# Three chunks instead of two taken in turns at the start of two stages, with later norm sums and fewer small VectorE operations

## The chip, the cores and the metric

The kernel runs on one core of a Trainium2 chip. The metric is the device time of one execution in microseconds; lower is better. The core's engines are named as in the profile: PE is TensorE (matrix products), PEld its weight loads, DVE is VectorE, ACT is ScalarE, POOL is GpSimd, and SP issues most of the transfers.

## What is computed

The reference is a chain of residual blocks on x of 256 tokens by 1024 channels, all in float32: a gated linear attention, a feed-forward network and a gated side input (PLE), then a differential attention, a second feed-forward network and PLE, then a short convolution and a blockwise attention (MoBA). The change touches the differential attention and the convolution. Cut to what matters:

```python
def diff_attn_mixer(h, pos, w_in, g_q, g_k, lam_q1, lam_k1, lam_q2, lam_k2, g_sub, w_out, lambda_init):
    q, k, v = split_cols(h @ w_in, [D_MODEL, D_MODEL, D_MODEL])
    q = rms_norm(q.reshape(bsz, seq, nh, 2, dh), g_q)
    k = rms_norm(k.reshape(bsz, seq, nh, 2, dh), g_k)
    ...
    lam = (jnp.exp(jnp.sum(lam_q1.astype(F32) * lam_k1.astype(F32)))
           - jnp.exp(jnp.sum(lam_q2.astype(F32) * lam_k2.astype(F32))) + lambda_init)
    ...
        s = jnp.einsum('bhtqd,bhtkd->bhtqk', q_blk, kt).astype(F32) * scale
        pr = jax.nn.softmax(s, axis=-1)
        a = pr[:, :, 0] - lam * pr[:, :, 1]
        return jnp.einsum('bhqk,bhkd->bhqd', a.astype(vt.dtype), vt)
    ...
    o = rms_norm(o, g_sub) * (1.0 - lambda_init)
    return o.reshape(bsz, seq, D_MODEL) @ w_out

def short_conv_mixer(h, w_in, conv_w, w_out):
    b_gate, c_gate, xv, z = jnp.split(h @ w_in, 4, axis=-1)
    u = c_gate * xv
    ...
    y = b_gate * conv * jax.nn.silu(z)
    return y @ w_out
```

`h` is `rms_norm` of the block's input each time: x times the inverse root of its mean square, times a gain. There are 8 heads of two halves of 64.

## The kernel before, in words

**Products.** Each matrix product in float32 is made of three on split numbers: the left and right side are cut into a high part (a cast, `whi`, `xh`) and the rest (`wlo`, `xl`), and high by high, high by low and low by high are summed in one bank (`mm3`, L222 to L225). A *chunk* is 256 output columns; its 1024 inputs are 8 groups of 128. A chunk is cut into two *halves* of four groups each, 24 matmuls of TensorE. A half is one unit of the list `seq`, and one *turn* of the program.

**A turn.** `turn` (L196) first does side work that is due, then calls `ahead` (L160): the transfer of a unit's weights on SP's queue (512 KB into one of four buffers `raw`), the cast to `whi` on ScalarE (L169), the subtract to `wlo` on VectorE (L178), four to five units ahead of their use; then more side work; then the 24 matmuls. Side work is kept in a heap by due time in turns; the delays stand in the table `DL`, by step name and, where a chunk or norm has its own, its number. Each engine carries out its instructions in the order in which the program issues them, so the table sets what stands behind what.

**Banks.** Three banks of the accumulator (pool `psg`, names `g`) hold chunks in work, five (`psm`, names `m`) all else. A chunk's bank is free when the engines that read it are done.

**The norm ahead of a stage.** The norm's gain is applied to the input at once, its inverse root only when a chunk is read out, so products start before the root is known. Each quarter i of the input (two groups of 128) gives `xh` (ScalarE, L301), `xl` (VectorE, L305), a square (ScalarE, L314) and sums of squares (L321 and L325 on GpSimd, L329 on VectorE). `fin` (L338, L343) sums over the channels with a matmul of ones; `root` (L348) loads ScalarE's table of exponential and logarithm and makes `rb` (and per token `rn`, `ev` at L357). The quarters come from the chunks of the PLE in front: its `done` (L453 reads the bank, a tanh at L457, a product with `pj` at L461, a sum `h` at L466). The differential attention's norm is number 3, the convolution's number 6.

**Order at a stage's beginning.** `woven` takes the first chunks in turns: first halves, then second halves. The second half of any chunk needs the last quarters of the input, which the last PLE chunk makes.

```python
    def woven(chunks, n=2):

        r = [u for p in zip(*chunks[:n]) for u in p]
        return r + [u for c in chunks[n:] for u in c]
```

**Differential attention** (`diff_plan`). Chunks q0, k0, q1, k1, q2, k2, v0, q3, k3, v1, v2, v3; a q or k chunk carries two heads. `qk_done` reads its bank: products with the tables `qcos` and `qsin` (or k's) on VectorE (L888, L893), their sum `ro` on GpSimd (L897), a square on ScalarE (L795), sums `ss` and `ms` on VectorE (L799, L801), their inverse root `r` on ScalarE (L282, L283). k is scaled by `r` on GpSimd (L901); for q, `r` is kept as two scaled copies `rqs` (L904, L905). Transposes on TensorE (L818) and a split into high and low (`kh` L823, `kl` L829) follow. `scores` takes a head through products on TensorE, a maximum (L941) and `nb` (L943) on VectorE, exponentials on ScalarE (L951), the weights `w` (L959 to L961) and the mix of the two softmaxes `e` (L968) on VectorE, transposes of it on TensorE (L975). `lam` makes the factor lambda, with the exponential `le` on ScalarE (L876) from VectorE's `ls` (L874).

**pT.** `proj_units` loads `pT` (128 rows of 512 numbers, 256 KB) for the second PLE's projection: one transfer on ScalarE's queue (L420), one cast to `px` (L427) and one subtract (L424).

**Convolution** (`conv_plan`). Sixteen chunks by the same `gemm` and `woven`; `cs` is the delay of a silu of the odd chunks.

Of the kernel before, what the change touches and what calls it, by code (L numbers as in the profile page):

```python
# [12 lines left out]
F32 = mybir.dt.float32  # L13
# [3 lines left out]
ALU = mybir.AluOpType  # L17
AX = mybir.AxisListType

P = 128  # L20
# [32 lines left out]
for _name, _n in (("ident", 128), ("dmask", 64)):  # L53
# [16 lines left out]
    "grm.2": 1.25, "grm.3": 1.75, "grh": 0, "grl": 0.75, "gload": 20.75, "dlam": 15.25, "dload": 24, "dqadd": 0,  # L70
    "dkadd": 0, "dqsq": 1, "dqred": 0, "dqrt": 0.75, "dqr": 0.5, "dqr.2": 1.25, "dqtr": 0, "dqhi": 0, "dqlo": 0.75,
    "dksq": 0, "dkred": 0, "dkrt": 0.75, "dkr": 0, "dktr": 1.25, "dkhi": 0, "dklo": 0.25, "dsc0": 0.75,
# [3 lines left out]
    "cs": 3.25, "cs.7": 2, "cy1": 0, "cy2": 0.75, "ch": 0, "cl": 2.25, "mqsq": 0, "mqred": 0.75, "mqrt": 0.5,  # L76
# [19 lines left out]
def body(ctx: ExitStack, tc: tile.TileContext, a, out: bass.AP):  # L96
# [269 lines left out]
    proj, hpj = {}, {}  # L366
# [108 lines left out]
    def ffn_plan(layer):  # L475
        p = 3 * layer + 1
        N = norms[p]
        S = SimpleNamespace(act={})

        def done(ps, f):  # L480
            g, sg, t3 = t1(), t1(), t1()
            nc.vector.tensor_mul(g, ps[:, 0], N.rb)  # L482
            if f < 8:
                if f % 2 == 0:
                    S.spare = new_x()
                ah, al = S.spare[0][:, f % 2], S.spare[1][:, f % 2]
            else:
                ah, al = [S.fp.tile([P, T], F32R, tag=n, name=n, bufs=FT - 8) for n in ("ah", "al")]

            def lo():  # L490
                nc.vector.tensor_sub(al, t3, ah.bitcast(F32))
                S.act[f] = (ah, al)

            chain(layer, ("fs", lambda: nc.scalar.activation(sg, g, AF.Silu)),  # L494
                  ("fm", lambda: nc.vector.tensor_mul(t3, sg, ps[:, 1])),
                  ("fh", lambda: nc.scalar.copy(ah, t3)),
                  ("fl", lo))

        ins = [gemm([("ffn_i", layer * FT + f, HALVES)], N.xs, lambda ps, f=f: done(ps, f)) for f in range(FT)]
        outs = [gemm([("ffn_o", (layer * 4 + i) * 3 + c, n) for c, n in enumerate((HALVES, HALVES, (4, 2)))], S.act,  # L500
                     lambda ps, i=i: add_h(p, i, ps, N.rb)) for i in range(4)]

        @contextmanager
        def room():
            with tc.tile_pool(name=f"ff{layer}", bufs=1) as S.fp:
                yield

        return woven(ins) + [u for c in outs for u in c], room
# [335 lines left out]
    def diff_plan():  # L844
        N = norms[3]
        S = SimpleNamespace(og={}, rq={}, qT={}, kT={}, aT={}, tabs={}, el={}, vd=set())
        load, proj_u = proj_units(1)
# [37 lines left out]
        def qk_done(ps, i, nm):  # L885
# [13 lines left out]
            def by_r():  # L899
                if nm == "k":  # L900
                    on("dkn").tensor_mul(units64(b.ro), units64(b.ro), per64(b.r))  # L901
                else:
                    sc = S.gt.tile([P, 2, 2, 4], F32, tag="rqs", name="rqs", bufs=3)
                    nc.vector.tensor_scalar(sc[:, 0], b.r, 0.125, None, op0=ALU.mult)  # L904
                    nc.vector.tensor_scalar(sc[:, 1], b.r, -0.125, None, op0=ALU.mult)  # L905
# [20 lines left out]
        def scores(h):  # L926
# [12 lines left out]
            def top(c):  # L939
                mx = tiny.tile([P, 2], F32, tag="mx", name="mx")  # L940
                nc.vector.tensor_reduce(mx, b.ps[c], axis=AX.X, op=ALU.max)  # L941
                nb = tiny.tile([P, 2], F32, tag="nb", name="nb", bufs=3)
                nc.vector.tensor_mul(nb, mx, S.rq[i][:, 1, :, 2 * hl + c])  # L943
                b.nb.append(nb)

            def exps(c):
# [3 lines left out]
                for t in range(2):  # L950
                    nc.scalar.activation(e[:, t], b.ps[c][:, t], AF.Exp, bias=b.nb[c][:, t:t + 1],  # L951
                                         scale=S.rq[i][:, 0, t, 2 * hl + c:2 * hl + c + 1],
# [3 lines left out]
            def weights():  # L956
# [3 lines left out]
                nc.vector.tensor_mul(b.w, b.w, b.l[:, 0])  # L960
                nc.vector.tensor_scalar(b.w, b.w, S.nlam, None, op0=ALU.mult)  # L961
# [72 lines left out]
        units = woven([q(0), k(0), q(1), k(1), q(2), k(2), v(0), q(3), k(3), v(1), v(2), v(3)])  # L1034
# [3 lines left out]
        def room():  # L1038
            with tc.tile_pool(name="diff", bufs=1) as S.gp, tc.tile_pool(name="difft", bufs=1) as S.gt:
                prepare()  # L1040
                at("dload", load)
# [5 lines left out]
    def conv_plan():  # L1047
        p = 6
# [67 lines left out]
        return ple_plan(1) + woven(chunks) + out_chunks("conv_o", S.ys, p, lambda: N.rb), room  # L1116
# [311 lines left out]
```

## Time and profile before

| | |
|---|---|
| median of 3 runs | 938.64 us (937.6 to 939.99) |
| the profiled execution's own time | 937.24 us |
| its span, first to last instruction | 935.1 us |
| mean granted clock of TensorE in it | 0.992 |
| instructions in the span | 19090 |

The span is the part that the views show; the 2.1 us around it are start and end. Times in the views count from the span's start. A wait is put down to the engine, tile and line that ended last of all that an instruction waited for. TensorE's instructions overlap, so a row's own duration is longer than the step from one start to the next.

### The profile page before, as it was taken

Reading aid. Unit: us, or ns where it says so; the run is one execution under the profiler, and the core shown is the slowest. Engines: PE = TensorE matmul, PEld = TensorE weight load, DVE = VectorE, ACT = ScalarE, POOL = GpSimd, SP = SyncE. Lnnn points to the kernel's source line nnn. Section 1 sums busy time; section 2 is a strip of 40 time slices with the busy share of each in tenths; the row PEclk is TensorE's granted clock in tenths of the full one; section 3 lists DMA queues with packets and bytes.
Section 4 is the critical chain, followed back from the end, with each engine's and each line's share of the span. In section 5 each row is a group of like instructions: output and inputs, shape, how many; then the busy total and the mean of one; then the engine's idle time right before and its main releaser. Section 6 shows DMA issues by size and latency. Waiting matters only on the chain.

```text
span 935.1 us, 19090 instructions
## 1 busy us (share of the span) xinstructions
PE 913.7 (98%) x7812; PEld 900.6 (96%) x7812; DVE 663.4 (71%) x1000; ACT 556.2 (59%) x951; POOL 107.3 (11%) x74
## 2 busy tenths in 40 slices
PE   9889999999999989899999999999999999999998
PEld 8889999999999989899999999999999999999998
DVE  5884768666656698998587666566897668876663
ACT  5945757455444565677585545444774445777862
POOL 0050310000001352211010000012210003000010
PEclk9989999999999998999999999999999999999999
DMA  8543366655555734343466555565556546644332
GB/s 243 200 138 107 109 205 230 211 189 195 181 189 190 241 127 149 122 141 108 146 217 215 199 193 193 177 200 195 168 206 201 192 132 205 186 134 136 113 114 90
DMA packets 48151, 161.10 MB, mean 172 GB/s; under 512 B 5472, under 2 KB 6368, under 8 KB 48064
## 3 DMA queue, kind: packets, MB, share of 16 engines
q1 hardware_dynamic: 47376, 158.81, 51.7%
q8 instruction: 61, 1.00, 0.4%
q10 hardware_dynamic: 688, 1.07, 0.4%
q14 instruction: 26, 0.21, 0.1%
HBM read 158.81 MB, written 1.05 MB: 171 GB/s over the span
## 4 chain that ended last, share of the span: by engine, by line
PE 81%; DVE 10%; ACT 4%; POOL 2%; issue 2%; DMA 2%; SPq 0%; ACTq 0%; POOLq 0%; DVEq 0%
PE g L223 25%; PE g L225 24%; PE g L224 24%; DVE wlo L178 3%; ACT whi L169 1%; PE m L223 1%; PE m L818 1%; DVE xl L305 1%; PE m L996 1%; DMA h<-in_xT 1%; PE m L1196 1%; PE m L653 1%; ACT xh L301 1%; PE m L224 1%; DVE q L600 1%
## 5 line engine op out<-in xcount | busy, mean ns | idle before, releaser
L223 PE MATMUL g<-xh,whi 128*128 128x256 f32 (+1 forms) x1672 | 465.7, 279 | 1.3 <-ACT whi L169 0.7
L225 PE MATMUL g<-xh,wlo 128*128 128x256 f32 (+1 forms) x1672 | 462.5, 277 | 0.2
L224 PE MATMUL g<-xl,whi 128*128 128x256 f32 (+1 forms) x1672 | 462.4, 277 | 0.1
L178 DVE TENSOR_TENSOR wlo<-raw,whi 128x1024 fp32r<-128x1024 f32 (+2 forms) x315 | 377.3, 1203 | 80.3 <-PE g L225 43.8
L169 ACT CAST whi<-raw 128x1024 fp32r<-128x1024 f32 (+2 forms) x315 | 312.0, 996 | 117.6 <-PE g L224 93.4
L223 PEld LDWEIGHTS g<-xh,whi 128*128 128x128 f32 (+1 forms) x1672 | 314.1, 188 | 2.4 <-ACT whi L169 1.0
L225 PEld LDWEIGHTS g<-xh,wlo 128*128 128x128 f32 (+1 forms) x1672 | 313.8, 188 | 0.6 <-DVE wlo L178 0.6
L224 PEld LDWEIGHTS g<-xl,whi 128*128 128x128 f32 (+1 forms) x1672 | 313.7, 188 | 0.6 <-DVE xl L305 0.3
L223 PE MATMUL g<-whi,xh 128*128 128x256 f32 x448 | 130.8, 292 | 3.5 <-ACT xh L301 3.5
L225 PE MATMUL g<-whi,xl 128*128 128x256 f32 x448 | 127.1, 284 | 0.2 <-DVE xl L305 0.2
L224 PE MATMUL g<-wlo,xh 128*128 128x256 f32 x448 | 126.9, 283 | 0.0
L223 PEld LDWEIGHTS g<-whi,xh 128*128 128x128 f32 x448 | 86.8, 194 | 5.2 <-ACT xh L301 4.0
L225 PEld LDWEIGHTS g<-whi,xl 128*128 128x128 f32 x448 | 86.6, 193 | 0.6 <-DVE xl L305 0.6
L224 PEld LDWEIGHTS g<-wlo,xh 128*128 128x128 f32 x448 | 86.5, 193 | 0.0
L494 ACT ACTIVATE t<-t 128x256 f32<-128x256 f32 x44 | 18.5, 420 | 85.7 <-DVE t L482 85.6
L223 PE MATMUL g<-ah,whi 128*128 128x256 f32 x224 | 61.8, 276 | 0.0
L224 PE MATMUL g<-al,whi 128*128 128x256 f32 x224 | 61.8, 276 | 0.0
L225 PE MATMUL g<-ah,wlo 128*128 128x256 f32 x224 | 61.8, 276 | 0.0
L482 DVE TENSOR_TENSOR t<-g,rb 128x256 f32<-128x256 f32 x44 | 18.6, 424 | 52.1 <-PE g L225 52.0
L305 DVE SCALAR_TENSOR_TENSOR xl<-h,small,xh 128x256 fp32r<-128x256 f32 x64 | 36.6, 610 | 17.1 <-ACT xh L301 17.1
L301 ACT ACTIVATE xh<-h,small 128x256 fp32r<-128x256 f32 x64 | 29.3, 503 | 32.1 <-DVE h L466 7.9
L379 POOL TENSOR_TENSOR h<-h,pj 128x512 f32<-128x512 f32 x8 | 12.9, 1621 | 276.6 <-DVE h L395 270.8
(224 smaller groups left out, 1010.0 us busy)
## 6 DMA issues: line engine op xcount, KB each, us to landing
raw<-in_ffn_i SPq DMA_DIRECT2D x88, 512.0 KB, 4.6
raw<-in_ffn_o SPq DMA_DIRECT2D x40, 512.0 KB, 4.0
raw<-in_conv_i SPq DMA_DIRECT2D x32, 512.0 KB, 4.6
raw<-in_moba_i SPq DMA_DIRECT2D x32, 512.0 KB, 3.8
raw<-in_diff_i SPq DMA_DIRECT2D x24, 512.0 KB, 3.8
raw<-in_gla_i SPq DMA_DIRECT2D x23, 512.0 KB, 5.1
raw<-in_ple_g SPq DMA_DIRECT2D x16, 512.0 KB, 4.7
raw<-in_gla_o SPq DMA_DIRECT2D x5, 512.0 KB, 4.0
```

What stands on the lines that cost most here:

```text
L169: nc.scalar.copy(hi[:, :kn * c], raws[u][:, :kn * c])
L178: nc.vector.tensor_sub(lo[:, :kn * c], raws.pop(u)[:, :kn * c], hi[:, :kn * c].bitcast(F32))
L223: nc.tensor.matmul(ps, lh, rh, start=first, stop=False, **kw)
L224: nc.tensor.matmul(ps, lh, rl, start=False, stop=False, **kw)
L225: nc.tensor.matmul(ps, ll, rh, start=False, stop=last, **kw)
L301: nc.scalar.activation(xh[:, j], h[:, j], AF.Copy, scale=gain[j])
L305: nc.vector.scalar_tensor_tensor(xl[:, j], h[:, j], gain[j], xh[:, j].bitcast(F32), op0=ALU.mult, op1=ALU.subtract)
L379: nc.gpsimd.tensor_add(n, h, proj[p // 3][i])
L482: nc.vector.tensor_mul(g, ps[:, 0], N.rb)
L494: chain(layer, ("fs", lambda: nc.scalar.activation(sg, g, AF.Silu)), ("fm", lambda: nc.vector.tensor_mul(t3, sg, ps[:, 1])), ("fh", lambda ...
L600: nc.vector.tensor_mul(Q[:, :, 0::2], q16.rearrange("p (m n) c -> p m n c", n=2), ep.rearrange("p (m n) c -> p m n c", n=2))
L653: nc.tensor.matmul(ps[:, d, :192], S.kk[d].rearrange("p (m n) c -> p m (n c)", n=2)[:, 2 * h + t], S.q3[d][:, 2 * h + t].rearrange("p n c ...
```

## The change

`woven` gets a third chunk in the differential attention (q0, k0 and q1) and in the convolution (the first three). `fin` of norms 3 and 6 is due a turn later. The load of `pT` for the second PLE, with its cast and subtract, is due 48 turns into the first feed-forward network, not 24 turns after the differential attention's beginning. Three delays move by a half or a whole turn. In the attention the maximum is taken with its sign turned, so that one copy of `rqs` serves for two; the two operations on `w` become one.

```diff
-"fin": 2, "fin.0": 1,
+"fin": 2, "fin.3": 3, "fin.6": 3, "fin.0": 1,
-"dload": 24,
+"dload": 48,
-"dsc0": 0.75, "dsc1": 1.75, "cs": 3.25, "cs.7": 2,
+"dsc0": 0.75, "dsc0.0": 1.25, "dsc1.0": 2.25, "dsc1": 1.75, "cs": 3.25, "cs.7": 2, "cs.0": 2.25,
...
@@ ffn_plan, room
             with tc.tile_pool(name=f"ff{layer}", bufs=1) as S.fp:
+                if layer == 0:
+                    at("dload", early["load"])
                 yield
@@ diff_plan
-        load, proj_u = proj_units(1)
+        early["load"], proj_u = proj_units(1)
...
-                    sc = S.gt.tile([P, 2, 2, 4], F32, tag="rqs", name="rqs", bufs=3)
-                    nc.vector.tensor_scalar(sc[:, 0], b.r, 0.125, None, op0=ALU.mult)
-                    nc.vector.tensor_scalar(sc[:, 1], b.r, -0.125, None, op0=ALU.mult)
+                    sc = S.gt.tile([P, 2, 4], F32, tag="rqs", name="rqs", bufs=3)
+                    nc.vector.tensor_scalar(sc, b.r, 0.125, None, op0=ALU.mult)
...
-                nc.vector.tensor_reduce(mx, b.ps[c], axis=AX.X, op=ALU.max)
+                nc.vector.tensor_reduce(mx, b.ps[c], axis=AX.X, op=ALU.max, negate=True)
...
                 nc.vector.reciprocal(b.w, b.l[:, 1])
-                nc.vector.tensor_mul(b.w, b.w, b.l[:, 0])
-                nc.vector.tensor_scalar(b.w, b.w, S.nlam, None, op0=ALU.mult)
+                nc.vector.scalar_tensor_tensor(b.w, b.w, S.nlam, b.l[:, 0], op0=ALU.mult, op1=ALU.mult)
...
-        units = woven([q(0), k(0), q(1), k(1), q(2), k(2), v(0), q(3), k(3), v(1), v(2), v(3)])
+        units = woven([q(0), k(0), q(1), k(1), q(2), k(2), v(0), q(3), k(3), v(1), v(2), v(3)], 3)
...
                 prepare()
-                at("dload", load)
                 yield
@@ conv_plan
-        return ple_plan(1) + woven(chunks) + out_chunks("conv_o", S.ys, p, lambda: N.rb), room
+        return ple_plan(1) + woven(chunks, 3) + out_chunks("conv_o", S.ys, p, lambda: N.rb), room
```

How the change moves instructions shows in the engines' queues. TensorE's, behind the two first halves of q0 and k0, before: `g_4333` is q0's bank and `g_4385` k0's, `m_4440` and `m_4442` the norm's sums; each half's 24 matmuls are cut to its first.

```order
L223 MATMUL g_4333<-whi_4237,xh_4292 128x256 [waits Activation_49]
L224 MATMUL g_4333<-wlo_4285,xh_4292 128x256 [waits DVE_49]
L225 MATMUL g_4333<-whi_4237,xl_4293 128x256 [waits DVE_49]
...
L338 MATMUL m_4440<-ssum_4301,ones_89 128x256 [waits DVE_49]
L343 MATMUL m_4442<-ones_89,ssum_4301 128x4 x2
L223 MATMUL g_4385<-whi_4283,xh_4292 128x256
```

And with the change, where `g_4422` is q1's bank, `g_4339` q0's and `g_4391` k0's:

```order
L223 MATMUL g_4422<-whi_4243,xh_4235 128x256 [waits DVE_49]
L224 MATMUL g_4422<-wlo_4291,xh_4235 128x256
L225 MATMUL g_4422<-whi_4243,xl_4236 128x256
...
L223 MATMUL g_4339<-whi_4289,xh_4298 128x256 [waits Activation_49]
L224 MATMUL g_4339<-wlo_4335,xh_4298 128x256
L225 MATMUL g_4339<-whi_4289,xl_4299 128x256
...
L338 MATMUL m_4477<-ssum_4307,ones_89 128x256 [waits DVE_49]
L343 MATMUL m_4479<-ones_89,ssum_4307 128x4 x2
L223 MATMUL g_4391<-whi_4333,xh_4298 128x256
```

q1's first half, on the first two quarters of the input, now stands ahead of q0's second half and waits for VectorE; the sum stands behind q0's second half as before, with one half more ahead of it.

ScalarE's queue around the root of the norm, before (`r_4549` belongs to q0, `r_4553` to k0; two products of the square at L795 stand between):

```order
L169 CAST whi<-raw 128x1024 x2
L348 ACT_TABLE_LOAD
...
L169 CAST whi<-raw 128x1024 x2
L795 ACTIVATE t_4529<-g 128x512
L795 ACTIVATE t_4537<-g 128x512
L169 CAST whi<-raw 128x1024
...
L283 ACTIVATE r_4549<-ln 128x8
...
L283 ACTIVATE r_4553<-ln 128x8
L876 ACTIVATE le<-ls 128x2
```

And with the change, whose lines 795 and 876 are 797 and 878:

```order
L169 CAST whi<-raw 128x1024 x3
L348 ACT_TABLE_LOAD
...
L169 CAST whi<-raw 128x1024 x2
L797 ACTIVATE t_4565<-g 128x512
L797 ACTIVATE t_4573<-g 128x512
L878 ACTIVATE le<-ls 128x2
L169 CAST whi<-raw 128x1024
...
L283 ACTIVATE r_4596<-ln 128x8
...
L283 ACTIVATE r_4600<-ln 128x8
```

Three casts, not two, stand ahead of the table load; `le` stands ahead of a cast and of the roots of q0 and k0, not behind them.

VectorE's queue around the same root, before:

```order
L329 TENSOR_TENSOR ssum<-ssum,sq 128x256 x2
L178 TENSOR_TENSOR wlo<-raw,whi 128x1024 x2
L357 TENSOR_SCALAR ev<-m 128x2
L178 TENSOR_TENSOR wlo<-raw,whi 128x1024
L888 TENSOR_TENSOR m<-g,qcos 128x512
L893 TENSOR_TENSOR m<-g,qsin 128x8x32 x2
```

And with the change:

```order
L329 TENSOR_TENSOR ssum<-ssum,sq 128x256 x2
L178 TENSOR_TENSOR wlo<-raw,whi 128x1024 x3
L357 TENSOR_SCALAR ev<-m 128x2
L178 TENSOR_TENSOR wlo<-raw,whi 128x1024
L890 TENSOR_TENSOR m<-g,qcos 128x512
L895 TENSOR_TENSOR m<-g,qsin 128x8x32 x2
```

One subtract more stands ahead of `ev`. From the first q product to the mix of head 2 (the third at L968) there are ten of these subtracts before and nine with the change.

## Rows read from the trace of the kernel before

**Rows 1.** The page, parts 1 and 2: engines' busy time, TensorE's clock by slices
```profile
PE 913.7 (98%) x7812; PEld 900.6 (96%) x7812; DVE 663.4 (71%) x1000; ACT 556.2 (59%) x951; POOL 107.3 (11%) x74
...
PEclk9989999999999998999999999999999999999999
```

**Rows 2.** Waits of TensorE, whole span: us in total, times, longest
```profile
PE g L223 <- ACT xh L301: 4.1, 3, 2.9
...
PE m L818 <- POOL ro L901: 1.9, 1, 1.9
...
PE m L224 <- DVE kl L829: 1.0, 1, 1.0
...
PE m L975 <- DVE e L968: 0.7, 1, 0.7
```

**Rows 3.** Timeline of TensorE, 338 to 352: start us, us, instruction [idle before <-releaser]
```profile
338.81 0.28 PE L223 MATMUL g<-whi,xh 128*128 128x256 f32 x1
...
345.76 0.28 PE L225 MATMUL g<-whi,xl 128*128 128x256 f32 x1
348.92 0.39 PE L223 MATMUL g<-whi,xh 128*128 128x256 f32 x1 [2.88 <-ACT xh L301]
...
350.89 1.17 PE L338 MATMUL m<-ssum,ones 128*128 128x256 f32 x2
```

**Rows 4.** Windows: us, busy us (instructions) by engine, granted clock, DMA, GB/s
```profile
350.50:357.30 6.80, 6.80 (x32) 6.58 (x31) 5.75 (x9) 5.53 (x9) 0.57 (x1) 0.50 0.54 184
```

**Rows 5.** Windows, the stretch behind it
```profile
355.30:401.54 46.24, 42.49 (x355) 40.63 (x354) 44.02 (x89) 28.88 (x69) 12.59 (x9) 0.98 0.39 127
```

**Rows 6.** Timeline of VectorE, 345 to 403
```profile
345.64 0.75 DVE L453 TENSOR_TENSOR t<-g,rb 128x256 f32<-128x256 f32 x2
...
354.17 1.22 DVE L178 TENSOR_TENSOR wlo<-raw,whi 128x1024 fp32r<-128x1024 f32 x1
355.30 0.68 DVE L888 TENSOR_TENSOR m<-g,qcos 128x512 f32<-128x512 f32 x1
...
399.95 1.66 DVE L968 SCALAR_TENSOR_TENSOR e<-e,w 128x256 f32<-128x256 f32 x2
```

**Rows 7.** Timeline of ScalarE, 349 to 353
```profile
349.70 1.98 ACT L169 CAST whi<-raw 128x1024 fp32r<-128x1024 f32 x2
351.69 1.28 ACT L348 ACT_TABLE_LOAD   x1
```

**Rows 8.** Groups of VectorE's instructions, 353 to 470: line, shapes, count | busy us, mean ns | idle
```profile
L961 DVE TENSOR_SCALAR w<-w,nlam 128x2 f32<-128x2 f32 x8 | 4.7, 584 | 0.3
...
L960 DVE TENSOR_TENSOR w<-w,l 128x2 f32<-128x2 f32 x8 | 1.3, 161 | 0.3
...
L905 DVE TENSOR_SCALAR rqs<-r 128x8 f32<-128x8 f32 x4 | 0.7, 162 | 0.0
```

**Rows 9.** Timeline of VectorE and GpSimd, 376 to 385
```profile
376.64 1.29 POOL L897 TENSOR_TENSOR ro<-m 128x512 f32<-128x512 f32 x1 [6.04 <-DVE w L959]
...
376.78 1.19 DVE L961 TENSOR_SCALAR w<-w,nlam 128x2 f32<-128x2 f32 x1
...
384.18 0.23 DVE L961 TENSOR_SCALAR w<-w,nlam 128x2 f32<-128x2 f32 x1
```

**Rows 10.** Timeline of TensorE and VectorE, 679 to 685, conv's beginning
```profile
679.03 0.75 DVE L453 TENSOR_TENSOR t<-g,rb 128x256 f32<-128x256 f32 x2
...
681.51 0.28 PE L225 MATMUL g<-xh,wlo 128*128 128x256 f32 x1
...
682.37 0.38 PE L223 MATMUL g<-xh,whi 128*128 128x256 f32 x1 [0.58 <-ACT xh L301]
...
684.28 0.70 PE L338 MATMUL m<-ssum,ones 128*128 128x256 f32 x2
```

**Rows 11.** Timeline of ScalarE, 362 to 366
```profile
362.79 0.21 ACT L283 ACTIVATE r<-ln 128x8 f32<-128x8 f32 x1
365.06 0.20 ACT L876 ACTIVATE le<-ls 128x2 f32<-128x2 f32 x1 [2.06 <-DVE ls L874]
```

More of the change, by code (lines that the diff above doesn't have):

```diff
@@ L69 @@
     "gon": 1.25, "gor": 0, "gom": 0, "grs.0": 4, "grs.1": 3, "grs.2": 2.75, "grs.3": 1, "grm.0": 1.5, "grm.1": 1.5,
-    "grm.2": 1.25, "grm.3": 1.75, "grh": 0, "grl": 0.75, "gload": 20.75, "dlam": 15.25, "dload": 24, "dqadd": 0,
+    "grm.2": 1.25, "grm.3": 1.75, "grh": 0, "grl": 0.75, "gload": 20.75, "dlam": 15.25, "dload": 48, "dqadd": 0,
     "dkadd": 0, "dqsq": 1, "dqred": 0, "dqrt": 0.75, "dqr": 0.5, "dqr.2": 1.25, "dqtr": 0, "dqhi": 0, "dqlo": 0.75,
-    "dksq": 0, "dkred": 0, "dkrt": 0.75, "dkr": 0, "dktr": 1.25, "dkhi": 0, "dklo": 0.25, "dsc0": 0.75,
+    "dksq": 0, "dkred": 0, "dkrt": 0.75, "dkr": 0, "dktr": 1.25, "dkhi": 0, "dklo": 0.25, "dsc0": 0.75, "dsc0.0": 1.25, "dsc1.0": 2.25,
     "dsc1": 1.75, "dp1": 0, "dt0": 0, "dt0.7": 0.25, "dt1": 0, "de0": 0.5, "de1": 0, "dw": 0.5, "dmix": 0.75,
@@ L75 @@
     "dored": 0, "dort": 0.5, "don": 0, "dotr": 1.25, "dohi": 0, "dolo": 0.25, "c0": 0, "c1": 1.75, "c2": 0,
-    "cs": 3.25, "cs.7": 2, "cy1": 0, "cy2": 0.75, "ch": 0, "cl": 2.25, "mqsq": 0, "mqred": 0.75, "mqrt": 0.5,
+    "cs": 3.25, "cs.7": 2, "cs.0": 2.25, "cy1": 0, "cy2": 0.75, "ch": 0, "cl": 2.25, "mqsq": 0, "mqred": 0.75, "mqrt": 0.5,
     "mqrt.0": 1.25, "mqn": 0.5, "mqtr": 0.75, "mqhi": 0.25, "mqlo": 1.25, "mksq": 0, "mkred": 0.25, "mkred.2": 0,
@@ L365, in body @@
     hs = [{} for _ in range(9)]
-    proj, hpj = {}, {}
+    proj, hpj, early = {}, {}, {}
     def give(p, i, h):
@@ L940, in top @@
                 mx = tiny.tile([P, 2], F32, tag="mx", name="mx")
-                nc.vector.tensor_reduce(mx, b.ps[c], axis=AX.X, op=ALU.max)
+                nc.vector.tensor_reduce(mx, b.ps[c], axis=AX.X, op=ALU.max, negate=True)
                 nb = tiny.tile([P, 2], F32, tag="nb", name="nb", bufs=3)
-                nc.vector.tensor_mul(nb, mx, S.rq[i][:, 1, :, 2 * hl + c])
+                nc.vector.tensor_mul(nb, mx, S.rq[i][:, :, 2 * hl + c])
                 b.nb.append(nb)
@@ L951, in exps @@
                     nc.scalar.activation(e[:, t], b.ps[c][:, t], AF.Exp, bias=b.nb[c][:, t:t + 1],
-                                         scale=S.rq[i][:, 0, t, 2 * hl + c:2 * hl + c + 1],
+                                         scale=S.rq[i][:, t, 2 * hl + c:2 * hl + c + 1],
                                          accum_out=b.l[:, c, t:t + 1])
```

2 rows, old and new, of the table DL are left out of this document.

## Prediction

> **What bounds the kernel now.** I read the engines and the clock by slices first, then TensorE's waits, then the two places that the change touches. TensorE is busy for 98% of the span, and two slices show a lower granted clock [rows 1]: time can only come from where TensorE stands or runs slowly. Of its waits, the largest, 2.9 us, is for ScalarE's `xh` (L301), and three shorter ones (1.9, 1.0, 0.7) are for GpSimd's `ro`, VectorE's `kl` and VectorE's `e` [rows 2]. TensorE's order of time puts the 2.9 where the differential attention begins: the two first halves of q0 and k0 run from 338.81, q0's second half stops after 345.76 and goes on at 348.92, since its last four inputs come from the last PLE chunk; the norm's sum stands at 350.89 [rows 3]. [...] From 355.30 to 401.54 another engine sets the pace: VectorE is busy for 44.02 of 46.24 us [rows 5]. The three shorter waits lie in it: TensorE is early there, and waits. So what TensorE wins before 355 reaches the end only as far as VectorE gets through its queue sooner.
>
> **The third first half.** Before, TensorE lost 348.92 - 345.76 = 3.16 us, 3.04 beyond one step of 0.118. Now q1's first half stands ahead of q0's second. It could start where two halves end, 338.81 + 48 x 0.118 = 344.47. But there are three banks, and q1 takes the one of the last PLE chunk, which VectorE reads out (L453) from 345.64 for 0.75 [rows 6]; in VectorE's queue all that stands ahead of this is unchanged. So the half waits some 2.0 us, starts at 346.45 and ends at 349.3 (24 x 0.118 = 2.83). By then `xh` is there (348.92 before), q0's second half runs through, and the sum comes at 352.1: four halves by 352.1, not three by 350.89, so TensorE is 2.83 - 1.2 = 1.6 us ahead. At most it wins 1.6, the 3.4 that the half clock cost (6.80 / 2), and the 3.6 of the shorter waits: 8.6. A part goes back at once, by my estimate under 1 us: with three chunks begun all three banks are taken until q0's is read out, and that ends after the first q products (356.25, below, with 0.68 and 0.75 for them, and ScalarE's square behind its casts), while k0 and q1 end at 352.4 + 2 x 2.83 = 358.1.
>
> **What VectorE makes of it.** Its first work on q0 waits for the norm's root, and that for ScalarE. There a cast more (1.98 for two, so 0.95 from start to start with overlap) stands ahead of the activation table load of 1.28 at 351.69 [rows 7]; that puts the load at 352.6, past the sum at 352.1 + 0.4. So `ev` and the first q product come 0.95 later, 356.25. Against this, to the mix of head 2 (399.95, the last that TensorE waits for here [rows 6]) the new queue has one `wlo` fewer: the third one is done before the root, where VectorE idles. That is 355.30 - 354.17 = 1.13. The trims: each q chunk loses one `rqs` (0.16), each head one of the two operations on `w` (0.16) [rows 8]; two and three of them stand ahead of head 2's mix, 0.80; one more of each ahead of k2's `kl`, 0.32. `negate` in the maximum adds an option, no instruction; its price no row shows: zero to 0.16 on each of 16 is its bound, and I take zero, since row for row a reduce costs its 512 elements. Sum: 0.95 - 1.13 - 0.80 - 0.32 = **-1.3 us**.
>
> **The merged operation on `w`.** At 376.78 the removed-in-part `w<-w,nlam` took 1.19, at 384.18 it took 0.23; the long one lies beside GpSimd's `ro`, 376.64 to 377.93 [rows 9]. Its mean of 584 ns over eight [rows 8] says that this happens several times. If the wait left with the operation, two of them by head 2, at 0.96 each, would bring 1.9 more; if the next operation inherits it, nothing. I take nothing: an `e` of 1.66 [rows 6] is stretched in the same way, and GpSimd's nine operations [rows 5] are the same as before. [...]
>
> **Conv.** The same edit a second time. From 681.51 to the norm's sum at 684.28 are 2.77 us for 13 steps of 0.118, 1.53: 1.24 is lost [rows 10]. The bank of the last PLE chunk is read out at 679.03 + 0.75 = 679.78, the third half would start 12 steps of 0.113 before 681.6, at 680.27: half a microsecond to spare, so no new wait. Behind it the root has one cast more ahead of it (0.95), but TensorE one half more to do (2.83), so c0's bank is read out in time; the list of waits has none on the conv's evacuations now. **-1.25 us**, between 0 (if the margin of 0.5 is eaten) and -1.24.
>
> **The rest.** The load, cast and subtract of `pT` move into the FFN: no wait of TensorE lies near either place in the list of waits, so 0; if that cover fails, a cast and a subtract, at most 1.5. Their DMA is 256 KB once on ScalarE's queue. Head 0's and 1's scores a half turn later, and a silu a turn sooner: the first waits behind VectorE anyway, 0.
>
> **Sum.** -1.3 - 1.25 = -2.55 on the profiled execution of 937.24, so 934.7. That execution lies 1.40 under the median of 938.64; so the forecast is **936.1 us**.
>
> **Rivals.**
> B: *VectorE meets GpSimd less often.* Of L961's 4.7 us, 8 x 0.23 = 1.8 is its own work and 2.9 waiting [rows 8, 9], and other operations wait too. The new order pairs other operations. If 3.0 goes, 937.24 - 5.55 + 1.40 = 933.1. For it: TensorE has 8.6 to give. Against: GpSimd's nine operations are the same and follow VectorE's products; they could as well meet more often. 0.23.
> C: *the clock falls anyway.* The stop of 2.88 was followed by 6.80 us at half clock [rows 3, 4], that of 0.58 in conv by none [rows 1, 10]. The new one of 2.0 lies between. If the clock falls by 349.3, q0's second half takes 5.7, the sum ends near 355.4, and the table load that hides it ends at 352.6 + 1.28 = 353.9: root and q0's product come 1.5 later still. VectorE's part becomes +0.2, the whole -1.05: 937.6. 0.17. [...]
> D, the slower side: *the lambda exponential holds ScalarE.* `le` now stands ahead of a cast and of both roots `r`. It waits for VectorE's `ls`: before, it ran at 365.06, after an idle 2.06, and r(k0) had been there since 362.79 + 0.21 [rows 11]. Now r(k0) comes near 366.1, 3 us later, and with it GpSimd's scaling of k0, its transposes, `kh`, `kl`, head 0's scores. This decides if `kh` (then 368.8) is later than VectorE's turn at `kl`; its queue gets there near 371, so some 2 us of slack speak against it. If it decides with the slack gone, VectorE idles for up to 3.2: its part becomes +1.9, the whole +0.65, 939.3; with C's 1.5 as well and nothing won in conv, 942.0. 0.10.
>
> **Numbers.** The forecast's case has 0.50, with -1.0 to -3.9 around its sum (conv at 0, or the two `w` waits gone with some more): 934.7 to 937.6. The range reaches into B and C: 932.0 to 939.4; B's far end and D's are left out. 0.3%, about what a measurement of this kernel can tell from no change, is 2.8 us: 935.8 and 941.5. Faster: all of B and two fifths of the forecast's case, 0.43. Slower: half of D, 0.05. The same: 0.52.
>
> **What would show it.** In the profile of the changed kernel: a wait of about 2.0 us on VectorE's L453 at 344.5, in place of 2.9 on `xh`; clock 1.00 from 350 to 358 (C: 0.50 again); a short wait for ScalarE's square of q0 near 358; table load near 352.6, q0's product near 356.3; VectorE still some 95% busy to 400, and TensorE's waits on `ro`, `kl` and `e` grown by several microseconds, as it is earlier and VectorE hardly is; no wait at conv's start. The forecast is wrong if TensorE goes past head 2's turn earlier than 399 (B), or later than 402 (C or D).

## The result and the profile after

The changed kernel took 930.64 us, median of five executions (929.29 to 932.95), against 937.6 for the kernel before (936.11 to 939.99): ratio 0.9923, 95% interval 0.9898 to 0.9948. It is 7.0 us faster; the forecast said 2.5, with 932.0 as the lower end. The profiled execution of it took 930.64 us, its span is 928.8. First its page (compare [rows 1]), then TensorE's waits (compare [rows 2]):

```profile
PE 912.7 (98%) x7812; PEld 900.6 (97%) x7812; DVE 658.0 (71%) x988; ACT 555.4 (60%) x951; POOL 106.5 (11%) x74
...
PEclk9899999999999999999999999999999999999999
```

```profile
PE m L975 <- DVE e L968: 2.5, 2, 1.8
PE g L223 <- DVE t L453: 1.8, 1, 1.8
...
PE m L820 <- POOL ro L903: 0.8, 1, 0.8
PE g L223 <- ACT xh L301: 0.7, 1, 0.7
PE g L223 <- ACT t L797: 0.2, 1, 0.2
```

The wait of 2.9 for `xh` is gone from the attention's beginning; a wait of 1.8 for VectorE's L453 has come, as forecast. The waits for `ro`, `kl` and `e`, forecast to grow by several microseconds, were 3.6 in all and are 3.3: `e` has grown from 0.7 to 2.5, `ro` has fallen from 1.9 to 0.8, `kl` is gone. That for ScalarE's square of q0 is new, 0.2, and the 0.7 for `xh` stands at MoBA's beginning. TensorE's row at the new wait and the norm's sum, VectorE's way through the block, then ScalarE's root and exponential (compare [rows 3, 6, 11]):

```profile
343.33 0.39 PE L223 MATMUL g<-whi,xh 128*128 128x256 f32 x1 [1.80 <-DVE t L453]
...
350.62 0.59 PE L338 MATMUL m<-ssum,ones 128*128 128x256 f32 x2
```

```profile
342.53 0.75 DVE L453 TENSOR_TENSOR t<-g,rb 128x256 f32<-128x256 f32 x2
...
353.57 0.68 DVE L890 TENSOR_TENSOR m<-g,qcos 128x512 f32<-128x512 f32 x1
...
389.06 1.25 DVE L962 SCALAR_TENSOR_TENSOR el<-l 128x2 f32<-128x2 f32 x1
...
393.76 1.66 DVE L968 SCALAR_TENSOR_TENSOR e<-e,w 128x256 f32<-128x256 f32 x2
```

```profile
349.54 1.28 ACT L348 ACT_TABLE_LOAD   x1
...
361.34 0.20 ACT L878 ACTIVATE le<-ls 128x2 f32<-128x2 f32 x1 [2.06 <-DVE ls L876]
...
362.96 0.21 ACT L283 ACTIVATE r<-ln 128x8 f32<-128x8 f32 x1
```

Two windows answer to [rows 4] and [rows 5]; the other two show where stretches of lower clock now lie (columns as there):

```profile
350.50:357.30 6.80, 6.63 (x57) 6.38 (x55) 4.34 (x8) 4.13 (x8) 2.21 (x1) 1.00 0.84 290
355.30:400.00 44.70, 41.18 (x339) 39.22 (x338) 41.84 (x88) 30.68 (x74) 12.30 (x9) 0.96 0.40 132
343.60:347.00 3.40, 3.40 (x18) 3.40 (x18) 3.05 (x7) 1.86 (x5) 0.94 (x2) 0.50 0.50 154
396.00:399.40 3.40, 3.40 (x22) 3.40 (x21) 3.40 (x6) 2.58 (x6) 0.00 (x0) 0.67 0.50 175
```

The clock is 1.00 from 350.5 to 357.3, but 0.50 from 343.6 to 347.0, while q1's first half runs. VectorE is still the busy engine behind it, 41.84 of 44.70.

To see where the time went I cut both traces at the last sum of squares of each norm (VectorE, L329), as this operation is there in all kernels. In microseconds, with the first four kernels of the next section beside them; "step" is the distance from one of TensorE's starts to the next in the long stretch of the stage, in nanoseconds:

| kernel | its time | norm 0 to 1, linear attention | 1 to 2, FFN0 | step | 3 to 4, attention | 4 to 5, FFN1 | step | 5 to 7, conv | step |
|---|---|---|---|---|---|---|---|---|---|
| before | 937.24 | 127.15 | 176.11 | 113 | 129.09 | 177.27 | 113 | 138.49 | 113 |
| the change | 930.64 | 123.97 | 176.88 | 113 | 127.32 | 177.09 | 113 | 137.11 | 113 |
| without conv | 942.47 | 125.24 | 176.25 | 113 | 125.97 | 183.97 | 118 | 142.79 | 118 |
| without the attention's third chunk | 938.17 | 123.85 | 182.60 | 118 | 128.61 | 177.06 | 113 | 137.11 | 113 |
| only the load | 937.36 | 124.37 | 176.69 | 113 | 128.36 | 177.30 | 113 | 142.11 | 118 |
| only the trims | 937.49 | 124.48 | 176.40 | 113 | 128.42 | 177.28 | 113 | 142.46 | 118 |

In the first two rows the attention gives 1.77 and conv 1.38, both near the forecast, but 3.2 come from the linear attention, whose instructions are the same in both kernels, and 0.7 from the start; FFN0 takes 0.8 more. In the kernel before, the clock was 0.50 from 60.4 to 67.2, in the linear attention; in the changed one it was so from about 26 to 33. Why it costs less there is not shown. The other rows told the rest.

### The profile page after: what moved, and what is told of

Same layout as the page of the kernel before. It is cut to its first block, busy times and chain, and to the rows that moved or that the text cites. A ratio compares the mean times of both kernels' runs of the same rounds, so it can differ in the third digit from the quotient of the medians.

```text
span 928.8 us, 19081 instructions
## 1 busy us (share of the span) xinstructions
PE 912.7 (98%) x7812; PEld 900.6 (97%) x7812; DVE 658.0 (71%) x988; ACT 555.4 (60%) x951; POOL 106.5 (11%) x74
## 4 chain that ended last, share of the span: by engine, by line
PE 87%; DVE 7%; POOL 2%; ACT 2%; DMA 1%; issue 1%; SPq 0%; DVEq 0%; ACTq 0%; POOLq 0%
PE g L223 26%; PE g L224 26%; PE g L225 26%; DVE wlo L178 2%; PE m L820 1%; PE m L223 1%; PE m L996 1%; PE m L1195 1%; DMA h<-in_xT 1%; ACT whi L169 1%; DMA raw<-in_ple_g 1%; PE m L655 1%; PE m L224 1%; DVE q L602 1%; DVE mx L942 1%
```

## The experiments

**Each part undone or alone.** The whole change without its part in conv:

```diff
-"fin.3": 3, "fin.6": 3,  ...  "cs.0": 2.25,
+"fin.3": 3,
-        return ple_plan(1) + woven(chunks, 3) + out_chunks(...)
+        return ple_plan(1) + woven(chunks) + out_chunks(...)
```

> The change without its part in the conv (two chunks in turns there, its norm's sum and one silu as before). Stages are measured from one norm's last sum of squares (VectorE, L329) to the next. In the two profiles at hand the change gains 1.8 us from norm 3 to norm 4 (the attention), 1.4 from norm 5 to norm 7 (the conv's beginning), nothing in the FFNs, and 3.9 ahead of norm 1, in the linear attention, whose instructions are the same in both. Theory F (two places, the rest is where a stretch of half clock happens to lie): this kernel is 1.4 slower than the whole change, from norm 3 to 4 as fast as it, and over many executions the whole change is some 3 to 4 faster than before, not 7. Theory G (the conv is worth more than its own stage shows, for the transfers behind it come sooner): 3 us or more slower than the whole change.

Median 933.5 (930.16 to 942.47) of 11 executions, 2.9 above the whole change (which ran in the first set of executions and the last, so that such distances carry the sets' own, up to 3.1 us between their medians of the kernel before); the ratio to before is 0.9956 (0.9932 to 0.9979). No theory had the spread of 12 us. The table has its cause: in the traced execution FFN1, which this edit does not touch, took 183.97 instead of 177, and conv 142.79, at a granted clock of 1.00.

The whole change without the third chunk in the attention:

```diff
-"fin.3": 3, "fin.6": 3,  ...  "dsc0.0": 1.25, "dsc1.0": 2.25,
+"fin.6": 3,
-        units = woven([...], 3)
+        units = woven([...])
```

> The change without the third chunk in the differential attention (order, norm sum and the two score delays there as before); VectorE's trims, the load and the conv's part stay. Theory F: conv's 1.4 stays, and of the attention's 1.8 what the trims give by themselves, 0.8 to 1.5; so 2.2 to 2.9 faster than before, 0.3 to 1.0 slower than the whole change. TensorE waits 2.9 us for xh again, with a stretch at half clock behind it. Rival H (the third first half and the clock it saves are what counts): under 1.6 faster than before, and the attention's stage as long as before.

Median 935.32 (931.34 to 938.17), ratio 0.9962 (0.9945 to 0.9978). The attention's stage is as long as before, 128.61: rival H holds there, the trims bring next to nothing without the third chunk. Its time does not hold: the median is 3.5 below before, not under 1.6. Conv keeps its 137.11. FFN0 is at 118 in the trace.

Only the load of `pT` moved (`"dload": 48`, issued in the FFN's room):

> Only the load of pT with its cast and subtract moved into the first FFN, all else as before. Theory F: nothing, within 0.5 us of before, FFN0's stage (norm 1 to norm 2) 176 to 177. Rival L (the transfer or the cast collides with the weights there, or frees the attention of a cast, a subtract and a transfer): over 1 us either way. It also gives a second look at the linear attention ahead of norm 1, with the instructions of before: 127.2 us from norm 0 to norm 1 again speaks for a fixed place of the half clock, 124 for chance.

Median 938.66 beside 938.78, ratio 1.0001 (0.9988 to 1.0014): nothing. The linear attention took 124.37 with the instructions of before. In fifteen traces that followed the first it lasted 123.85 to 127.22, whatever the kernel; it is chance.

Only VectorE's trims (the diff's lines at `rqs`, `negate` and `w`):

> Only VectorE's trims in the attention (one scaled copy of the root instead of two, the maximum with its sign turned, two operations on w in one), all else as before. Theory F, as forecast: VectorE is the bound there, so 0.16 for each of 3 rqs and 4 w that stand ahead: 1.1 us in the attention's stage; the wait for GpSimd that the second operation on w had (1.19 against 0.23) is taken over by the next one. Rival W (the wait goes with the operation): 2 us or more. Rival N (VectorE's queue is not the bound, the third chunk is): under 0.4.

Median 935.51 (933.95 to 944.8), ratio 0.9972 (0.9952 to 0.9992), 3.3 less than before, and yet the attention's stage is 128.42 and the mix of head 2 comes 49.6 us after the norm's last sum of squares, where the three traces of weave by two without trims have 49.3 to 50.1. The merged operation itself takes 0.22, and its neighbour inherits the wait: VectorE's timeline of this kernel shows `el` beside GpSimd's `ro` (373.75 to 375.07), and a later one without.

```profile
373.69 0.22 DVE L959 SCALAR_TENSOR_TENSOR w<-w,nlam,l 128x2 f32<-128x2 f32 x1
373.83 1.26 DVE L960 SCALAR_TENSOR_TENSOR el<-l 128x2 f32<-128x2 f32 x1
...
381.11 0.16 DVE L960 SCALAR_TENSOR_TENSOR el<-l 128x2 f32<-128x2 f32 x1
```

So the trims' 3.3 us did not come from the attention.

**The step of the matmuls.** All windows here are 50 us of conv, the columns as above; the granted clock is 1.00 in each and the engine never idle, but the number of matmul rows in it is either 444 or 427. First the kernel before, then the trims alone, then the change:

```profile
700.00:750.00 50.00, 50.00 (x444) 50.00 (x443) 35.66 (x60) 23.82 (x33) 0.00 (x0) 1.00 0.60 199
```

```profile
700.00:750.00 50.00, 50.00 (x427) 50.00 (x426) 34.52 (x60) 23.35 (x33) 0.00 (x0) 1.00 0.58 190
```

```profile
700.00:750.00 50.00, 50.00 (x443) 50.00 (x443) 36.84 (x61) 24.75 (x34) 0.00 (x0) 1.00 0.60 199
```

Two rows of TensorE in that stretch of the kernel before, and of a second execution of the same kernel (its run follows), show the step itself, 0.11 and 0.12 in these digits:

```profile
700.13 0.28 PE L223 MATMUL g<-xh,whi 128*128 128x256 f32 x1
700.24 0.28 PE L224 MATMUL g<-xl,whi 128*128 128x256 f32 x1
```

```profile
700.04 0.28 PE L223 MATMUL g<-xh,whi 128*128 128x256 f32 x1
700.16 0.28 PE L224 MATMUL g<-xl,whi 128*128 128x256 f32 x1
```

A stretch mostly keeps its step: in FFN1 of the kernel before, all 1,508 steps from 484 to 655 are of 113 or 114 ns. Conv has some 900 matmuls behind its norm's sum, 4.4 ns each is 4 us; an FFN has 1,583, 7 us. To see whether the step belongs to the program or to the execution, two unchanged kernels ran again, for a trace each. The kernel before:

> The kernel before, unchanged, for a second trace. In the traces so far TensorE's steps in an undisturbed stretch are either 113 or 118 ns at the same granted clock of 1.00, and a stretch keeps its step until something comes between. Theory P (the step is drawn where TensorE stands still for a norm's sum; where the sum is ready, the stretch behind it runs at 113): the conv behind norm 6, whose sum TensorE waits for, lasts 111.4 us at 113 or some 115.0 at 118, and time goes with it: up to 937.3 with 111.4, 937.3 or more with 115.0. Theory Q (the step belongs to the program, by where its code and buffers lie): 111.4 as in the first trace. The linear attention: 124 or 127, by where the half clock falls.

936.8 us, conv 142.11 at 118, the linear attention 124.42. The kernel before is the same; conv's step is not. The trims alone:

> VectorE's trims alone, unchanged, for a second trace: the first had the conv at 118 (115.0 us) and 937.5 us, but nine of its other ten executions took 934.0 to 936.1. Theory P: an execution at 934 to 936 shows the conv at 113, 111.4 us, and nothing else that differs by more than 1.5 us. Theory Q: 118 again, and the difference must lie elsewhere. The attention's stage is 128.4 as in the first trace, that is, the trims bring nothing there, in either.

933.17 us, conv 138.88 at 113, the attention 127.77, the linear attention 124.15. The same kernel, 4.3 us apart, 3.6 of it conv. Theory Q falls as it was put: one program can run at either step.

What decides? In [rows 10] TensorE stands still for `xh` and is held up again, by some 0.01 us, for the norm's sum; the second trace of the kernel before has the same, here with VectorE's last sum, which ends at 680.02 for a matmul at 680.07:

```profile
678.15 0.38 PE L223 MATMUL g<-xh,whi 128*128 128x256 f32 x1 [0.59 <-ACT xh L301]
...
680.07 0.70 PE L338 MATMUL m<-ssum,ones 128*128 128x256 f32 x2
```

```profile
679.13 0.89 DVE L329 TENSOR_TENSOR ssum<-ssum,sq 128x256 f32<-128x256 f32 x2
```

In the changed kernel the sum of norm 6 stands a half later. VectorE has it at 679.55, and TensorE comes to it in its stride:

```profile
680.56 0.28 PE L225 MATMUL g<-xh,wlo 128*128 128x256 f32 x1
680.67 0.59 PE L338 MATMUL m<-ssum,ones 128*128 128x256 f32 x2
```

```profile
678.66 0.89 DVE L329 TENSOR_TENSOR ssum<-ssum,sq 128x256 f32<-128x256 f32 x2 [0.46 <-ACT sq L314]
```

Then I counted over all 16 traces, for the sums of the five norms that have a long stretch behind them. Where TensorE came to the sum in its stride at 113 (the sum 115 or 116 ns after the matmul before it), the stretch behind began at 113: 64 of 64; one of these did not stay there (below). Of the other 16, six were at 118 already when the sum came: four stayed, two went on at 113. In ten TensorE stood still for the sum, or came to it 117 to 139 ns after the matmul before: the stretch behind ran at 118 in seven and at 113 in three. Ahead of conv's sum TensorE also stops for `xh` in six traces; between the two stops the step is 113 in five of them, and three of these turn to 118 at the second. Two kernels were made so that TensorE stands still. The whole change with conv's sum a turn earlier:

```diff
-"fin.3": 3, "fin.6": 3,
+"fin.3": 3,
```

> The whole change, with norm 6's sum a turn earlier (the delay of two turns as before, three chunks in turns kept). TensorE ends the third first half some 1.6 us before the sum's input is ready and stands still for it, as it does in the kernel before. Theory P: the step behind it is drawn; conv's two stages together (137.1 in the whole change) are 138.5 to 139 at 113 or 142.5 to 143 at 118, and the executions fall into groups 4 us apart, their median 2 to 5 above the whole change. Theory Q: 1.6 more, in all executions.

The trace has a wait of 1.5 us for the sum and conv at 118, 142.47 us:

```profile
700.00:750.00 50.00, 50.00 (x427) 50.00 (x426) 34.87 (x60) 23.45 (x32) 0.00 (x0) 1.00 0.58 191
```

The 12 executions: six from 930.40 to 932.86, one at 934.14, four from 935.93 to 937.65, one at 940.8; median 933.5. Groups with one between them, and a median 2.9 above the whole change (ratio to before 0.9973, 0.995 to 0.9996): P, against Q's constant 1.6. And the FFNs' sums a turn earlier:

```diff
+"fin.1": 1, "fin.4": 1,
```

> The whole change, with the sums of norms 1 and 4, ahead of the FFNs, a turn earlier. Their inputs are ready 0.5 to 1.1 us before TensorE asks for them now; a half (2.7 us) earlier it stands still some 1.6 to 2.2 us for each, 3 to 4 in all, and part of that comes back since the root is there sooner. Theory P: each FFN's step is drawn; an FFN at 118 takes 184 instead of 177 us, so that executions spread over up to 14 us and the median is 3 to 12 above the whole change. Theory Q: 3 to 4 more at most, and both FFNs at 113.

Median 944.23 (938.92 to 949.16), ratio 1.0092 (1.0062 to 1.0121). TensorE waited 4.2 us for three sums; of the two FFNs one was drawn at 118 (186.94, with a stretch of lower clock in it) and one at 113 (179.21):

```profile
PE m L338 <- DVE ssum L329: 4.2, 3, 2.3
```

```profile
200.00:250.00 50.00, 50.00 (x427) 50.00 (x426) 31.56 (x45) 25.35 (x36) 0.00 (x0) 1.00 0.56 185
520.00:570.00 50.00, 50.00 (x443) 50.00 (x443) 31.26 (x45) 25.33 (x36) 0.00 (x0) 1.00 0.59 192
```

FFNs that are at 113 in 27 of the 30 stretches of the other traces were put at risk by a wait alone. Conv, whose order here is that of the change, met its sum in stride in this trace, 1.46 us after it was ready, and yet took 140.31: it ran at 113 up to a chunk's first matmuls, and at 118 behind them.

```profile
706.96 0.28 PE L225 MATMUL g<-xh,wlo 128*128 128x256 f32 x1
707.09 0.36 PE L223 MATMUL g<-xh,whi 128*128 128x256 f32 x1
707.28 0.28 PE L224 MATMUL g<-xl,whi 128*128 128x256 f32 x1
```

```profile
720.00:770.00 50.00, 50.00 (x427) 50.00 (x426) 33.42 (x56) 22.59 (x30) 0.00 (x0) 1.00 0.55 184
```

So the later sum makes 118 rarer, it does not rule it out: of the nine traces with conv in the changed order this is the one that ran at 118, of the seven with a stop at conv's sum five did. What makes the draw fall one way or the other stays open; its odds differ from set to set, and from kernel to kernel within a set: beside the first experiments one of 34 executions of the kernel before lies below 936.2, none of 12 with only the load moved, and nine of 11 with only the trims. The program has a share in the odds, then, and which part of it is not known. The kernel before ran in five sets, with medians of 937.6, 938.78, 935.64, 937.08 and 937.66. In the last, 23 executions, six lie between 932.85 and 934.69, 17 between 936.95 and 940.85, none between: the size of the gap fits conv's 3.6, and the mean granted clock is the same in both groups (0.993 to 0.996 and 0.992 to 0.996). In the set of 34 beside the first experiments 33 lie at 937.55 or more.

**The same edit at other places.** Three chunks in turns and the sum a turn later, ahead of both FFNs:

```diff
+"fin.1": 3, "fin.4": 3,
-        return woven(ins) + [...]
+        return woven(ins, 3) + [...]
```

> The whole change, and the same edit ahead of both FFNs: three chunks in turns, the sums of norms 1 and 4 a turn later. There TensorE does not stop now; the sum's input is ready 0.1 to 1.1 us before it. Theory P: the margin grows by a half, to some 3 us, so no execution has an FFN at 118 (184 instead of 177); the median the same as of the whole change or up to 1 lower, since an FFN was drawn at 118 in one trace of nine whose margin was under 0.2. Rival K (with three banks taken the third chunk's successor waits for the first bank): 1 to 2 us lost at each FFN, so 2 to 4 slower.

Median 932.77 (929.61 to 939.52), ratio 0.9975 (0.995 to 1.0): nothing won, and the sum is not all. FFN0 ran at 118 though its sum had been ready for 3.4 us:

```profile
200.00:250.00 50.00, 50.00 (x427) 50.00 (x427) 30.99 (x46) 24.73 (x36) 0.00 (x0) 1.00 0.57 186
```

It had been at 118 since 138.77, the first row of the third chunk's first half, which came 0.24 us after the row before it instead of 0.11 (rows of TensorE's timeline):

```profile
138.41 0.28 PE L224 MATMUL g<-xl,whi 128*128 128x256 f32 x1
138.53 0.28 PE L225 MATMUL g<-xh,wlo 128*128 128x256 f32 x1
138.77 0.36 PE L223 MATMUL g<-xh,whi 128*128 128x256 f32 x1
...
139.08 0.28 PE L225 MATMUL g<-xh,wlo 128*128 128x256 f32 x1
139.19 0.28 PE L223 MATMUL g<-xh,whi 128*128 128x256 f32 x1
```

So here too a hesitation, of 0.12 us, between two matmuls redrew the step, and the sum, met without a stop, passed it on.

In MoBA, and then in all places at once:

```diff
+"fin.7": 3,
-        units = woven([q[0], ..., v[3]] + z)
+        units = woven([q[0], ..., v[3]] + z, 3)
```

> The whole change, and the same edit in MoBA: three chunks in turns, the sum of norm 7 a turn later. TensorE stops there for xh (0.7) and for the sum (0.5): 1.2 us. MoBA from norm 7 to the end lasts 140.2 to 140.5 in nine traces, at either step behind the sum, since transposes and scores soon come between. Theory P: -1.2, no groups. Rival K (three banks, one load of ScalarE's table and one cast more ahead of the root): 0 to +2.

> The whole change, with the edit at the FFNs and in MoBA, both. Theory P: the sum of the two, -1 to -2 against the whole change, with the narrowest spread of all. Rival K: slower than the whole change by 2 or more.

Medians 934.86 and 935.15, ratios 0.9979 (0.9957 to 1.0001) and 1.0004 (0.9984 to 1.0023): rival K, and more than its 2 us. MoBA takes 144.4 in both instead of 140.2 to 140.5. TensorE waits where nothing waited in the kernel that it starts from, here in the first of the two:

```profile
PE g L223 <- DVE t L405: 2.2, 1, 2.2
...
PE g L223 <- DVE n L1138: 0.9, 1, 0.9
```

**The trims within the third chunk's order.** The whole change with the trims undone:

> The whole change without VectorE's trims (two scaled copies of the root, two operations on w). Theory from the runs with trims alone (they moved GpSimd's wait from the second operation on w to the next, el, 1.11 us, and the stage by less than its spread): the attention's stage stays at 126 to 127.3, VectorE reaches the mix of head 2 at most 1.0 later than the 46.5 to 47.0 us after the norm's last sum of squares that the whole change needs (50.06 before), and loses some 3.3 to GpSimd on the way, as with the trims. Rival (the trims carry what the third chunk seems to bring): 48.5 or more, and 6 to 7 lost to GpSimd.

Median 933.5 (930.98 to 937.62), ratio 0.9977 (0.9957 to 0.9997). The mix of head 2 comes 47.0 us after the norm's last sum, with the trims 46.5 to 47.0 in seven traces; the stage is 126.46, within the 125.3 to 127.3 of the kernels with the third chunk and the trims so far (128.55 in one with two stretches of lower clock in it). The third chunk carries the gain; the trims are worth half a microsecond there at most. The median is 2.9 above the change's all the same, in another set of executions; but for the 0.35 around the span (below), where the rest comes from is open. One `w` is long again, 1.18, and its `el` short:

```profile
392.13 1.18 DVE L963 TENSOR_SCALAR w<-w,nlam 128x2 f32<-128x2 f32 x1
393.22 0.15 DVE L964 SCALAR_TENSOR_TENSOR el<-l 128x2 f32<-128x2 f32 x1
```

**The bank's wait, and the whole change again.** The last chunk of each PLE read out a turn sooner, the sums at the same place in TensorE's order:

```diff
-"fin.3": 3, "fin.6": 3,
+"fin.3": 4, "fin.6": 4,
-        return woven([gemm([("ple_g", layer * 4 + i, HALVES)], N.xs, lambda ps, i=i: done(ps, i))
+        return woven([gemm([("ple_g", layer * 4 + i, HALVES)], N.xs, lambda ps, i=i: done(ps, i), late=1 if i == 3 else "done")
```

> The whole change, with the last chunk of each PLE read out a turn sooner (before, not behind, the next subtract on VectorE and cast on ScalarE, 1.2 us), the sums of norms 3 and 6 at the place they have now in TensorE's order. Theory: what is left of the stop at the attention's beginning is TensorE's wait of 1.8 us for that chunk's bank; it falls to some 0.6, and the last xh, the norm's sum and the root come 1.0 to 1.2 sooner, while VectorE still needs some 40.2 from q0's product to the mix of head 2: the attention, from norm 2 to norm 4, 1.0 to 1.2 shorter, conv unchanged at 113. Rival R (VectorE or ScalarE now stand still for TensorE's last PLE matmul, or the weights come late for want of the subtract): 0 to 1 slower.

Median 937.74, ratio 1.0009 (0.9989 to 1.0029): as slow as before. Counted from norm 2's last sum of squares, L453 came 1.13 us sooner than in the second trace of the change (below), as meant, but the subtract that it had overtaken came late, and TensorE stood still for `wlo` instead:

```profile
PE g L224 <- DVE wlo L178: 2.7, 1, 2.7
```

ScalarE then stood idle for 3.67 us for a cast's transfer, ahead of the root's table load, and the attention took 130.62. The wait of 1.8 us at the bank costs less than this way of taking it out. And the change unchanged:

> The whole change, unchanged, for a second trace and more executions beside those of before. Theory P: conv's two stages again 137.1 at 113, since its norm's sum is ready over 1 us before TensorE asks; the attention's stage 125.3 to 126.7 if no stretch of half clock falls into it (the first trace had one at 396 to 399, and 127.3); the linear attention 124 or 127, as in either kernel. Theory Q (the step is luck there too): 142.5 as often as not. The executions: 929 to 933, with few above 935.

Median 931.18 of 12 (928.04 to 937.2) beside 937.66: ratio 0.9935 (0.9914 to 0.9956). Conv 137.11 at 113 again. The attention 127.14, again with a stretch of lower clock from 396 on, which the kernels built on it mostly lack (125.3 to 126.7). By their medians none of the versions tried here beats the changed kernel itself.

## Why the prediction was wrong

Two steps failed. In the sum, the norm's sum in conv was priced as a wait only, and one trace of the kernel before stood for all its executions; by the account below that is where the time left the range. And GpSimd's collisions were put at nothing, which left the way to head 2's mix 2.1 us too long. Term by term:

*TensorE at the attention's beginning: the wait right, the clock in part C's.* The wait for L453 was forecast as 2.0 and is 1.8. The clock did not fall behind it as it had, but around it, for 3.4 us, in both traces of the change and in none of the seven others with the third chunk where L453 stands as it did. So the norm's sum comes 3.8 and 3.7 us after the norm's last sum of squares, where 2.2 was forecast (352.1 - 349.89) and 2.1 to 2.3 measured in the seven. What TensorE gives back for q0's bank was estimated as under 1 us: it is 0.2 and 0.3 in the change, 1.3 to 2.5 in the seven; VectorE comes to head 2's mix no later for it (46.5 to 47.0 us after its last sum of squares in six of the seven).

*VectorE's late start: right but for that.* ScalarE's table load was forecast 2.7 us after the norm's last sum of squares (352.6 - 349.89) and came 2.74 after it, 349.54. The first q product was to come 6.36 us after the norm's last sum of squares (356.25 - 349.89). It is 6.36 or 6.37 in seven traces with three chunks, 6.77 and 6.65 in the two of the change: of the 1.5 that C gave to the clock, 0.3 to 0.4 arrive.

*One subtract fewer, the trims: the subtract right, the trims too high.* There are nine subtracts on the way, as forecast. The trims were given 1.1 us and bring 0.5 at most. `negate` cost nothing, as taken: the maximum took 684 ns on average over 16 in both kernels. The wait for GpSimd passes to the next operation, as the text took it to: `el` at 389.06 is long, 1.25, in place of `w` in [rows 9].

*GpSimd's collisions: wrong, rival B.* The step "I take nothing: [...] GpSimd's nine operations [rows 5] are the same as before" failed. From the first q product to the mix of head 2 VectorE lost 6.1 and 5.3 us in the two traces of the kernel before to operations over 0.1 us longer than the shortest of their kind, 5.3 to 6.4 in the four others with two chunks in turns, and 2.4 to 2.6 in the kernels with three. The nine operations of GpSimd are there; more of them now fall beside VectorE's operations that are not stretched. GpSimd's scaling of k0 and of k1 in the change, and what VectorE did then, a q product and a maximum of the usual length:

```profile
363.31 1.04 POOL L903 TENSOR_TENSOR ro<-ro,r 128x512 f32<-128x512 f32 x1 [3.35 <-ACT r L283]
...
372.66 1.12 POOL L903 TENSOR_TENSOR ro<-ro,r 128x512 f32<-128x512 f32 x1 [1.08 <-ACT r L283]
```

```profile
363.04 0.69 DVE L890 TENSOR_TENSOR m<-g,qcos 128x512 f32<-128x512 f32 x1
...
372.80 0.68 DVE L942 TENSOR_REDUCE mx<-m 128x2 f32<-128x512 f32 x1
```

VectorE comes to that mix 3.1 us sooner, 46.96 us after the norm's last sum of squares instead of 50.06; the forecast had 1.0 (0.95 - 1.13 - 0.80). By the clock of the kernel before this is 396.9, earlier than the 399 that was to speak for B. Stretched beside GpSimd are `lm` (1.14 in the kernel before, 0.28 in the change), `wlo` (2.33 at most beside a shortest of 1.21, before), `e` (1.27 beside 0.47, the change), `el` (1.25 beside 0.15, the change) and `w<-w,nlam` [rows 9], though not each time; products out of the accumulator are not (0.68 and 0.69 for those with `qcos`, beside GpSimd and away from it). What sets the two apart no run tested. The 3.1 do not arrive whole: the stage was 1.77 shorter in the first pair of traces, and over all 128.5 on average with two chunks, 127.2 in the change's two traces, so 1.2 (126.3 in the seven others with three). The forecast's 1.3 for the stage is right by its sum and not by its reasons; that the two met is luck.

*Conv: the stop right, what hangs on it missed.* 1.25 forecast, 1.38 measured between traces at the same step. But the forecast priced the norm's sum as a wait only. In the kernel before TensorE stands still for it, and the step of the 900 matmuls behind it is drawn: 113 in the trace that I read, 118 in the next, and by the executions' groups in most of them. In the change it is met in stride, and the step was 113 in both traces; of the seven kernels built on it with the same order one ran at 118. A draw of 118 costs an execution of the kernel before 3.6 us. The clue was in the rows: the text used 0.118 and 0.113 for conv in neighbouring sentences [rows 10], at the same clock, and did not ask.

*The median: wrong base.* The profiled execution at 937.24 hid both things: conv at 113, which is 3.6 better than the next trace, and lower clock in the linear attention, which is 3 worse. They cancel, so it looked like a typical execution.

So the 7.0 us are, by what the traces show, some 1.2 in the attention, 1.4 at conv's stop, 0.35 around the span (below), and for the rest of about 4 the step in conv and the place of the half clock. How these last two divide is not settled, nor how much of either the change itself brought: the shares differ from set to set. The load was rightly priced at nothing. C came only in part (above), D did not: `le` ran at 361.34, r(k0) at 362.96, and VectorE reached `kl` of k0 13.47 us after the first q product, 13.46 before.

## What to carry to other kernels

When a long unbroken stretch of matmuls runs on one engine, look at the distance from start to start in each stage, not only at the granted clock, and take a second trace of the unchanged kernel before forecasting from one: 4% of a stage hung here on a hesitation at its beginning. A small operation in the middle of the stream cost little here when its operand had long been ready (the sum in the change's conv took 0.44 us of TensorE: from 680.56 to the second product behind it are 0.66, not two steps of 0.113), and put one half too early it went with a slower stretch behind it (1.5 us of wait, and conv at 142.47 instead of 137.11). And a reordering that leaves every instruction in place can still change what VectorE and GpSimd do beside each other (VectorE lost 5.3 to 6.4 us on the way to head 2's mix with two chunks in turns, 2.4 to 2.6 with three); price that by the longest and the shortest of each kind, and give it room on both sides.

## What the runs showed of the hardware that was not expected

- Matmuls of 128x256 in float32 products follow at 113.3 or 117.8 ns at a granted clock of 1.00, for up to 180 us on end. Where the roles of weights and input change, from the PLE's to the attention's chunks, 113.3 turns into 117.8 without a stop between, at 338.81 in the kernel before and at 335.71 in the change; two more such places in each of the two traces show the same, in the kernel before at 39.64 and 785.47.
- The time around the span was 1.75 to 1.87 us in all twelve traces of kernels with the trims and 2.14 to 2.20 in the four without. Twelve instructions fewer on VectorE (1000 and 988 on the pages) go with 0.35 us outside the profiled span; why is open.
- The place of the lower clock (0.50) in the linear attention changes from one execution to the next: between 26 and 34 alone in 12 traces, where the stage takes 123.9 to 125.5 us, from 60 to 67 in the first trace of the kernel before, and at both places in three, where it takes 126.4 to 127.2.
